# One plain feed-forward round per layer instead of two, with the output projection's accumulators held open between two passes

## The chip, the cores and the metric

The kernel runs on one core of a Trainium2 chip. The metric is the device time of one execution in microseconds (us); three executions of the kernel before took 1064.5 to 1064.76 us, median 1064.71 us. All times below are us from the start of the profiled span. PE is the matrix engine (TensorE), PEld its weight loads, DVE the vector engine (VectorE), ACT the scalar engine (ScalarE), POOL is GpSimd, SP the engine that issues most transfers.

## The reference, cut to what matters

Two identical layers run over one sequence of 512 frames of width 1024. A layer mixes three attention-like groups, projects their concatenated output back, and then applies a feed-forward of width 4096 with a squared ReLU:

```
x = x + concat(A, B, C) @ w_out
u = rms(x, norm2) @ w_ff1
x = x + square(relu(u)) @ w_ff2
```

with `rms(x, g) = x * rsqrt(mean(x*x) + 1e-6) * g`. Everything is float32. The change touches `concat(A, B, C) @ w_out` and the two feed-forward products.

## The kernel before

The activation `xT` lies transposed in SBUF: eight tiles of 128 features by 512 frames. Each float32 matrix product is made of three passes at a reduced input format: an operand is split into `hi` (a rounded copy) and `lo` (operand minus `hi`), and `mm3` (L262 to L265) issues hi·hi, hi·lo and lo·hi into one PSUM accumulator. For weights the split happens on the way: a weight tile of 128 x 1024 is loaded into a raw buffer, ACT copies it to `whi` (L205) and DVE writes `wlo = raw - whi` (L206). `jobs` is the list of weight tiles in the order of their use; `getjob` hands out the next, and `prep_ahead` prepares at most three (`HIB`) ahead, since `whi` and `wlo` have three buffers each: the copy for tile n waits until PE is done with tile n-3.

**Output projection** (`big_work`, L571 to L592). Its eight contraction tiles k are taken in three passes (`WPASS`: k 0 to 3, 4 and 5, 6 and 7), because the mixed output `yg` becomes ready in that order: tiles 6 and 7 come last, from `c_tail(0)` and `c_tail(1)`, which transpose `yts` (L1007, written by POOL at L1000) and split it. Each pass runs over four pairs of output tiles (`hf` 0 to 3) with two accumulators, and each accumulator is added into `xT` by DVE at the end of its pass (L587). After the last pass `xprep` writes `xh` and `xl`, the split, scaled input of the feed-forward (ACT L334, DVE L335). So one layer has 24 of the additions at L587.

**Feed-forward** (L1097 to L1383). The first matrix is taken in eight rounds of 512 output features. The first `NSTD` = 2 rounds are plain (`ff1_std`): four weight tiles per round, 48 matmuls of 128 x 256 each (8 pairs of k and feature half, two halves of the frames, three passes), 192 in all. The other rounds are Strassen-Winograd rounds (`ff1_st`): seven products of 24 matmuls each, 168 in all, from seven combinations of four weight blocks (`ORDER` = A11, S1, S2, A12, S4, S3, A22) and of the input's four blocks. S1 and S3 are summed by a second transfer that accumulates into the raw buffer (POOL's queue), S2 and S4 by DVE (L216, L220). The input's combinations are the tile `xbx`, written by `xsums` (ACT L354 and L363, DVE L356 to L375). A round ends with four blocks of squared ReLU in `ct`, whose combinations are split into `gx` and `yg` units for the second matrix (`csplit`, `n1_`, `n2_`, `tail_`; L1183 to L1205). Those of `tail_` are put off until the next round has begun (`late`, `flush`). The second matrix (`ff2`) uses Winograd products throughout, 14 for each pair of rounds, and adds each product into `xT` (`acc`, L1294). `ff_pairs` alternates one product of `ff2` with one of `ff1_st`. While the plain rounds run, `sqacc` sums the squares of `xT`, `xsums` runs, and `emit_r2` (L1121) makes the frame's normaliser: one all-ones matmul (L1123), then `nv`, Ln, Exp, and two DVE operations of a Newton step (L1130, L1131).

A scheduler fixes the order of the instructions on each engine when the program is built; each engine then runs its own list strictly in order.

## Time and profile before

| what | before |
|---|---|
| median of three runs | 1064.71 us |
| profiled execution, its own time | 1064.91 us |
| its span | 1063.1 us |
| PE instructions | 8768 matmuls |
| DMA moved | 151.86 MB |
| mean granted PE clock | 0.999 of full speed |

The span of the profiled execution is 1.8 us shorter than its time, and the execution took 0.2 us longer than the median. In layer 0 the output projection ends and the first plain round begins at about 222.7 us, the second plain round ends at about 267.2 us, and the feed-forward ends at about 546 us; layer 1 repeats the same stages some 525 us later. A busy share of PE counts pipelined matmuls that overlap, so it says that PE was never empty, not that it worked at its peak.

### The profile page before, as it was taken

The numbers are of one execution on the slowest core, as the hardware profiler recorded it, in microseconds if no ns is written. First come the engines' busy times: TensorE is split into PE (matmuls) and PEld (weight loads), VectorE is DVE, ScalarE is ACT, GpSimd is POOL, SyncE is SP. The second block draws the span as 40 slices with busy tenths as digits, with TensorE's granted clock in tenths as the row PEclk, the third lists the DMA queues.
The fourth block names the chain that finished last, engine by engine and source line by source line (L and its number), as shares of the span: only waits on it lengthen the run. The fifth ranks groups of instructions, "written<-read, shape, count | busy, mean of one in ns | idle before, by whom it ended". The sixth has DMA issues, their size and how long they took to land.

```text
span 1063.1 us, 21688 instructions
## 1 busy us (share of the span) xinstructions
PE 1054.7 (99%) x8768; PEld 1004.3 (94%) x8768; DVE 904.4 (85%) x1541; ACT 627.8 (59%) x1097; POOL 102.5 (10%) x154
## 2 busy tenths in 40 slices
PE   9999999999999999999999999999999999999998
PEld 8999977899999999999999998778999999999998
DVE  7696877899997988988977978678999888898898
ACT  6446655376666666567455467444766666666662
POOL 2030020100010000010001200101000101001000
PEclk9999999999999999999999999999999999999999
DMA  6523111165388677677135221213544877777742
GB/s 217 165 98 110 60 68 51 61 194 144 119 213 220 162 219 198 177 199 199 51 110 163 96 80 41 84 47 127 152 120 138 220 187 201 219 188 184 224 128 80
DMA packets 47365, 151.86 MB, mean 143 GB/s; under 512 B 5648, under 2 KB 8848, under 8 KB 47264
## 3 DMA queue, kind: packets, MB, share of 16 engines
q1 hardware_dynamic: 39056, 120.84, 33.8%
q0 software_dynamic: 8064, 29.36, 15.7%
q8 instruction: 69, 1.13, 0.4%
q14 instruction: 32, 0.26, 0.1%
q10 hardware_dynamic: 144, 0.26, 0.1%
HBM read 147.86 MB, written 2.13 MB: 141 GB/s over the span
## 4 chain that ended last, share of the span: by engine, by line
PE 86%; DVE 9%; ACT 3%; issue 1%; DMA 0%; SPq 0%; DVEq 0%
PE at L263 26%; PE at L264 26%; PE at L265 26%; DVE rt L726 2%; DVE wlo L206 2%; PE at L856 1%; PE at L898 1%; PE at L881 1%; ACT pe L769 1%; PE at L979 1%; DVE z L722 1%; DVE z L728 1%; PE at L756 1%; DMA raw<-in_w_in_dram 0%; DVE rb L407 0%
## 5 line engine op out<-in xcount | busy, mean ns | idle before, releaser
L205 ACT ACTIVATE whi<-raw 128x1024 fp32r<-128x1024 f32 (+1 forms) x130 | 136.2, 1048 | 114.3 <-PE at L264 87.3
L264 PE MATMUL at<-xhl,whi 128*128 128x256 f32 (+1 forms) x704 | 198.0, 281 | 0.0
L263 PE MATMUL at<-xhl,whi 128*128 128x256 f32 (+1 forms) x640 | 181.4, 283 | 0.0
L265 PE MATMUL at<-xhl,wlo 128*128 128x256 f32 (+1 forms) x640 | 180.4, 282 | 0.0
L206 DVE TENSOR_TENSOR wlo<-raw,whi 128x1024 fp32r<-128x1024 f32 (+1 forms) x130 | 157.2, 1209 | 26.8 <-ACT whi L205 26.5
L263 PE MATMUL at<-yg,whi 128*128 128x256 f32 (+1 forms) x592 | 179.8, 307 | 0.0
L265 PE MATMUL at<-yg,wlo 128*128 128x256 f32 (+1 forms) x592 | 178.4, 301 | 0.0
L264 PE MATMUL at<-yg,whi 128*128 128x256 f32 (+1 forms) x560 | 169.4, 303 | 0.0
L263 PE MATMUL at<-whi,xhl 128*128 128x256 f32 (+1 forms) x576 | 163.7, 284 | 0.2 <-ACT whi L205 0.2
L264 PE MATMUL at<-wlo,xhl 128*128 128x256 f32 (+1 forms) x576 | 161.2, 280 | 0.3 <-DVE wlo L206 0.3
L265 PE MATMUL at<-whi,xhl 128*128 128x256 f32 (+1 forms) x576 | 161.0, 280 | 0.1
L205 ACT ACTIVATE whi<-fraw 128x1024 fp32r<-128x1024 f32 x100 | 106.1, 1061 | 83.8 <-PE at L264 79.6
L206 DVE TENSOR_TENSOR wlo<-fraw,whi 128x1024 fp32r<-128x1024 f32 x100 | 121.9, 1219 | 26.2 <-ACT whi L205 25.7
L264 PEld LDWEIGHTS at<-xhl,whi 128*128 128x128 f32 x704 | 132.2, 188 | 1.8 <-issue 0.5
L263 PEld LDWEIGHTS at<-xhl,whi 128*128 128x128 f32 x640 | 120.2, 188 | 1.7 <-ACT ct L1232 0.5
L265 PEld LDWEIGHTS at<-xhl,wlo 128*128 128x128 f32 x640 | 120.1, 188 | 1.2
L263 PEld LDWEIGHTS at<-yg,whi 128*128 128x128 f32 x592 | 111.2, 188 | 5.6 <-issue 1.7
L265 PEld LDWEIGHTS at<-yg,wlo 128*128 128x128 f32 x592 | 111.1, 188 | 5.3
L263 PEld LDWEIGHTS at<-whi,xhl 128*128 128x128 f32 x576 | 109.1, 189 | 1.1 <-ACT whi L205 0.5
L264 PEld LDWEIGHTS at<-wlo,xhl 128*128 128x128 f32 x576 | 109.0, 189 | 0.6 <-DVE wlo L206 0.6
L265 PEld LDWEIGHTS at<-whi,xhl 128*128 128x128 f32 x576 | 109.1, 189 | 0.3 <-DVE xhl L335 0.3
L264 PEld LDWEIGHTS at<-yg,whi 128*128 128x128 f32 x560 | 105.2, 188 | 4.2 <-DVE yg L1009 0.5
(301 smaller groups left out, 2516.3 us busy)
## 6 DMA issues: line engine op xcount, KB each, us to landing
fraw<-in_w_dram SPq DMA_DIRECT2D x72, 512.0 KB, 4.4
raw<-in_w_dram SPq DMA_DIRECT2D x56, 512.0 KB, 4.3
raw<-in_w_in_dram SPq DMA_DIRECT2D x34, 512.0 KB, 3.3
fraw<-in_w_dram POOLq DMA_DIRECT2D x32, 512.0 KB, 6.5
raw<-in_w_out_dram SPq DMA_DIRECT2D x16, 512.0 KB, 3.2
xt<-in_w_dram SPq DMA_DIRECT2D x16, 512.0 KB, 6.0
raw<-in_w_dram POOLq DMA_DIRECT2D x14, 512.0 KB, 7.4
ms<-in_w_dram SPq DMA_DIRECT2D x12, 512.0 KB, 4.4
```

The costliest lines, as they stand in the source:

```text
L205: A.activation(hi[:, cs_], raw[:, cs_], AF.Copy)
L206: V.tensor_tensor(lo[:, cs_], raw[:, cs_], hi[:, cs_], ALU.subtract)
L263: T.matmul(o, sh, mh, start=first, stop=False, skip_group_check=skip)
L264: T.matmul(o, sh, ml, start=False, stop=False, skip_group_check=skip)
L265: T.matmul(o, sl, mh, start=False, stop=last, skip_group_check=skip)
L722: V.tensor_tensor(z10, z10, bc(rq), ALU.mult)
L726: V.tensor_tensor(r10[:, oo:oo + n, a:a + 32], z10[:, oo:oo + n, b:b + 32], tb(S_, n, a, a + 32), ALU.mult)
L728: V.tensor_tensor(zaq[t], ro[:, :640], rt[:, :640], ALU.add)
L756: T.matmul(sc[r][:, g * 256:g * 256 + nk], qTA[g][r * 64:(r + 1) * 64, c * P:(c + 1) * P], kTA[r * 64:(r + 1) * 64, k0:k0 + nk], start=Tru ...
L769: A.activation(pe[:, u, :nk], sc[u % 2][:, (u // 2) * 256:(u // 2) * 256 + nk], AF.Exp, bias=nmx[:, u:u + 1], accum_out=ssum[:, u:u + 1])
L856: T.matmul(sp[:, :nk], qTB[rs, pr, n * P:(n + 1) * P], kTB[rs, pr, :nk], start=True, stop=False)
L881: T.transpose(pt[:, b * P:(b + 1) * P], scs[r][:, b * P:(b + 1) * P], ident)
```

## The change

`NSTD` goes from 2 to 1 and `LEAD` from 0 to 7: the second round of each layer is now a Winograd round, and its seven products are all taken ahead of the first product of `ff2`. The work that lay beside the two plain rounds is dealt out anew: `xsums` runs in the four steps of the one plain round, `sqacc` and `emit_r2` are taken in the Winograd round that follows, and the two Newton operations move to `finish_r2`, at the end of the first `ff2`. The square of the plain round's second half no longer stands behind its ReLU but in `flush`, which the Winograd round calls after it has copied a bank (`A.activation(Y, X, AF.Copy)`); with the square go `n2_` and the release of the units. `bank(True)` picks a bank that has held a matmul before.

```
-NSTD = 2
+NSTD = 1
...
-    LEAD = 0
+    LEAD = 7
...
+            open_ = {}
+            for hf in range(3):
+                open_[hf] = [att() for _ in range(2)]
+                if hf != 1:
+                    ws = getjob()
+                for k in (4, 5):
+                    wo_part(open_[hf], ws[2 * (hf % 2) + k - 4], k, k == 4, False)
+                    if k == 5:
+                        done.add(f"wo1{hf}")
                     yield 1.31
+            for hf in (2, 0, 1, 3):
+                if hf == 3:
+                    open_[hf] = [att() for _ in range(2)]
+                if hf in (0, 3):
+                    ws = getjob()
+                for k in range(4 if hf == 3 else 6, 8):
+                    wo_part(open_[hf], ws[k - 4 if hf == 3 else (hf if hf < 2 else 1) * 2 + k - 6], k, hf == 3 and k == 4,
+                            k == 7)
...
+                wo_out(open_[hf], hf, True)
...
-        fill_to("wo1")
+        fill_to("wo11")
         c_tail(1)
+        fill_to("wo12")
         close_phase()
...
+        def finish_r2():
+            nv, lnv, r2 = (rr_[n] for n in ("nv", "lnv", "r2"))
             V.tensor_tensor(lnv, nv, r2, ALU.mult)
             V.scalar_tensor_tensor(r2, lnv, 2.0, r2, ALU.add, ALU.mult)
-            rr_.update(nv=nv, r2=r2)
...
+        def square(i):
+            A.activation(ct[:, 2 * i:2 * i + 2], ct[:, 2 * i:2 * i + 2], AF.Square)
+
         def flush():
             while late:
-                tail_(*late.pop(0))
+                s, rr, plain = late.pop(0)
+                if plain:
+                    square(1)
+                    if rr == NSTD - 1:
+                        units.extend(quads)
+                    n2_(s, rr)
+                tail_(s, rr)
...
-        for n_ in range(4 * NSTD):
-            next(gens[1])
+        for n_, (which, u) in enumerate([(1, None)] * 4 * NSTD + list(ff_pairs())):
+            next(gens[which])
             if n_ == 0:
+                xt_ = wt("xt", "xt")
+                bg = xsums(l, *(v3(xt_[:, i * S:(i + 1) * S], 256) for i in range(2)))
+            if n_ < 4:
+                next(bg)
+                next(bg)
+            if n_ == 4:
                 for kx in range(KT):
                     sqacc(kx, kx == 0)
-            if n_ == 3:
+                free_ff.append(xt_)
+            if n_ == 7:
                 emit_r2()
```

In the projection the first pass stays. Pass two now leaves the accumulators of `hf` 0, 1 and 2 open (six of the eight banks), pass three goes on in them in the order 2, 0, 1, and `hf` 3 takes its four contraction tiles in one go at the end. Three pairs are so added into `xT` once instead of twice: 18 additions per layer instead of 24. The host packs the weight tiles of `w_out` to match.

**Order on PE at the projection.** PE's list of layer 0 around the transposes of the last mixed tile (`yt` of `c_tail(1)`); `at` are PSUM banks, `yg` the mixed output, the number behind `whi` is the weight tile. Before:

```order
L263 MATMUL at_521_2838<-yg_91,whi_476_2624 128x512
L264 MATMUL at_521_2838<-yg_91,whi_476_2624 128x512
L265 MATMUL at_521_2838<-yg_91,wlo_477_2625 128x512
L1007 MATMUL at_522_2853<-ident_76,yt_493_2695 128x128 x4
L263 MATMUL at_530_2870<-yg_91,whi_512_2781 128x512
```

Now, 24 matmuls nearer to the program's start:

```order
L264 MATMUL at_515_2799<-yg_91,whi_419_2442 128x512
L265 MATMUL at_515_2799<-yg_91,wlo_420_2443 128x512
L1035 MATMUL at_516_2812<-ident_76,yt_493_2695 128x128 x4
L263 MATMUL at_517_2819<-yg_91,whi_476_2624 128x512
L264 MATMUL at_517_2819<-yg_91,whi_476_2624 128x512
```

The four transposes stood behind the second pass's last matmul with tile 476; they now stand ahead of its first.

**Order on DVE behind the plain rounds.** DVE's list of layer 0 from the last operation of `xsums` but one to the lo copies of the products that follow (`wlo` with the number of its tile, `ct` the blocks of the squared ReLU, `gx` and `yg` the units). Before, around the end of the first of two plain rounds:

```order
L206 TENSOR_TENSOR wlo_561_3253<-fraw_529_2869,whi_560_3252 128x1024
L356 SCALAR_TENSOR_TENSOR xbx_526_2866<-xt_555_3103,xbx_526_2866 128x512
L1199 SCALAR_TENSOR_TENSOR ct_528_2868<-ct_528_2868 128x512
L1200 TENSOR_TENSOR ct_528_2868<-ct_528_2868 128x512
L1184 TENSOR_TENSOR gx_527_2867<-ct_528_2868,gx_527_2867 128x1024 x2
L1130 TENSOR_TENSOR ms_525_2865<-ms_525_2865,r20_3237 128x512
L1205 SCALAR_TENSOR_TENSOR ct_528_2868<-ct_528_2868 128x512
L1131 SCALAR_TENSOR_TENSOR r20_3237<-ms_525_2865,r20_3237 128x512
L375 SCALAR_TENSOR_TENSOR xt_555_3103<-xT_89,pcol_106,xt_555_3103 128x256 x2
L1184 TENSOR_TENSOR yg_91<-ct_528_2868,gx_527_2867 128x1024
L356 SCALAR_TENSOR_TENSOR xbx_526_2866<-xt_555_3103,xbx_526_2866 128x512
L206 TENSOR_TENSOR wlo_563_3320<-raw0_73,whi_562_3319 128x1024
```

Now, around the end of the one plain round:

```order
L356 SCALAR_TENSOR_TENSOR xbx_524_2843<-xt_544_3013,xbx_524_2843 128x512
L206 TENSOR_TENSOR wlo_552_3217<-fraw_527_2846,whi_551_3216 128x1024
L1236 SCALAR_TENSOR_TENSOR ct_526_2845<-ct_526_2845 128x512
L1237 TENSOR_TENSOR ct_526_2845<-ct_526_2845 128x512
L206 TENSOR_TENSOR wlo_555_3275<-raw0_73,whi_554_3274 128x1024
L1221 TENSOR_TENSOR gx_525_2844<-ct_526_2845,gx_525_2844 128x1024 x2
L220 TENSOR_TENSOR fraw_527_2846<-raw0_73,fraw_527_2846 128x1024
L1242 SCALAR_TENSOR_TENSOR ct_526_2845<-ct_526_2845 128x512
L206 TENSOR_TENSOR wlo_557_3305<-fraw_527_2846,whi_556_3304 128x1024
L1221 TENSOR_TENSOR yg_91<-ct_526_2845,gx_525_2844 128x1024
L206 TENSOR_TENSOR wlo_559_3337<-raw2_75,whi_558_3336 128x1024
```

Between two halves of the same `ct` work there stood no lo copy before; now there are three, and a sum of weight blocks (L220), because the tiles are used up twice as fast. In both lists `L1236`/`L1199` and the two rows behind the first of them are the work of `n2_`, the rest of the `ct` rows that of `tail_`.

**Order on PE at the first product of `ff2`.** PE's list of layer 0 where the Winograd round ends (tile 562 is the first of `ff2`, tile 560 the last of the round):

```order
L264 MATMUL at_541_2957<-yg_91,whi_562_3408 128x256
L265 MATMUL at_541_2957<-yg_91,wlo_563_3409 128x256
L263 MATMUL at_541_2957<-yg_91,whi_562_3408 128x256
L264 MATMUL at_541_2957<-yg_91,whi_562_3408 128x256
L263 MATMUL at_538_2954<-xbx_524_2843,whi_560_3374 128x256
```

The scheduler has put the first 17 matmuls of the first `ff2` product ahead of the round's seventh product, and the other seven behind it.

More of the change, by code (lines that the diff above doesn't have):

```diff
@@ L572, in big_work, with wo_part @@
                 yield 1.31
-            for pi, (a, b) in enumerate(WPASS):
-                for hf in range(4):
-                    ps = [att() for _ in range(2)]
-                    if b - a == 4 or hf % 2 == 0:
-                        ws = getjob()
-                    for k in range(a, b):
-                        hi, lo = ws[k - a if b - a == 4 else hf % 2 * 2 + k - a]
-                        for j in range(2):
-                            cs_ = slice(j * P, (j + 1) * P)
-                            mm3(ps[j], hi[:, cs_], lo[:, cs_], yhi(k), ylo(k), k == a, k == b - 1)
-                        if k < b - 1:
-                            yield 1.31
-                    for j in range(2):
-                        kx = hf * 2 + j
-                        V.tensor_tensor(xT[:, kx], ps[j], xT[:, kx], ALU.add)
-                        if pi == len(WPASS) - 1:
-                            xprep(kx, g2(l, kx), xh, xl)
-                    if hf == 3:
-                        done.add(f"wo{pi}")
-                    yield 1.31
+            def wo_part(ps, tiles, k, first, stop):
+                hi, lo = tiles
+                for j in range(2):
+                    cs_ = slice(j * P, (j + 1) * P)
+                    mm3(ps[j], hi[:, cs_], lo[:, cs_], yhi(k), ylo(k), first, stop)
@@ new lines, in wo_out @@
+            def wo_out(ps, hf, full):
+                for j in range(2):
+                    kx = hf * 2 + j
+                    V.tensor_tensor(xT[:, kx], ps[j], xT[:, kx], ALU.add)
+                    if full:
+                        xprep(kx, g2(l, kx), xh, xl)
+            for hf in range(4):
+                ps = [att() for _ in range(2)]
+                ws = getjob()
+                for k in range(4):
+                    wo_part(ps, ws[k], k, k == 0, k == 3)
+                    if k < 3:
+                        yield 1.31
+                wo_out(ps, hf, False)
+                if hf == 3:
+                    done.add("wo0")
+                yield 1.31
@@ L1114, in trunk, with bank @@
         banks = deque(att() for _ in range(8))
-        def bank():
-            return banks.popleft()
+        full = set()
+        def bank(seeded=False):
+            b = next(b for b in banks if not seeded or id(b) in full)
+            banks.remove(b)
+            full.add(id(b))
+            return b
         rr_ = {}
@@ L1233, in ff1_std @@
                         banks.extend(ps)
-                        A.activation(ct[:, 2 * i:2 * i + 2], ct[:, 2 * i:2 * i + 2], AF.Square)
                         if i == 0:
+                            square(0)
                             csplit(s, rr)
@@ L1238, in ff1_std @@
                         else:
-                            if rr:
-                                units.extend(quads)
-                            n2_(s, rr)
-                            late.append((s, rr))
+                            late.append((s, rr, True))
                     yield
         def ff1_st(s, rr):
-            X, Y = bank(), bank()
+            X, Y = bank(), bank(True)
             prod1(X, 0)
@@ L1276, in ff1_st @@
             banks.append(X)
-            late.append((s, rr))
+            late.append((s, rr, False))
             if (s, rr) == (NS - 1, 1):
@@ L1359, in ff2 @@
                 if s == 0 and dg:
+                    finish_r2()
                     free_ff.append(ms_)
@@ L1365, in trunk @@
         bg = None
-        for n_ in range(4 * NSTD):
-            next(gens[1])
+        for n_, (which, u) in enumerate([(1, None)] * 4 * NSTD + list(ff_pairs())):
+            next(gens[which])
             if n_ == 0:
+                xt_ = wt("xt", "xt")
[4 more added lines that the diff above has]
+            if n_ == 4:
                 for kx in range(KT):
                     sqacc(kx, kx == 0)
-            if n_ == 3:
+                free_ff.append(xt_)
+            if n_ == 7:
                 emit_r2()
-            if n_ == 1:
-                xt_ = wt("xt", "xt")
-                bg = xsums(l, *(v3(xt_[:, i * S:(i + 1) * S], 256) for i in range(2)))
-            if bg is not None:
-                next(bg, None)
-                next(bg, None)
-        free_ff.append(xt_)
-        for which, u in ff_pairs():
-            next(gens[which])
         close_phase()
@@ L1417, in _layout @@
         c = w_out[l].reshape(D, 4, 256).transpose(1, 0, 2)
-        t = [tiles(c, a, b - a) for a, b in WPASS]
-        wo.append(cc([t[0]] + [cc([t_[0::2], t_[1::2]], 2) for t_ in t[1:]], 0))
+        t, u, v = (tiles(c, a, b - a) for a, b in WPASS)
+        two = [cc(p, 1) for p in ((u[0], u[1]), (u[2], v[2]), (v[0], v[1]), (u[3], v[3]))]
+        wo.append(cc([t, np.stack(two)], 0))
     wo = np.stack(wo)
```

8 lines of the change are left out of this document (added).

## The prediction

> **What bounds the kernel now.** I read the page first, for the engine that fills the span.
>
> ```profile
> PE 1054.7 (99%) x8768; PEld 1004.3 (94%) x8768; DVE 904.4 (85%) x1541; ACT 627.8 (59%) x1097; POOL 102.5 (10%) x154
> PE 86%; DVE 9%; ACT 3%; issue 1%; DMA 0%; SPq 0%; DVEq 0%
> ```
>
> PE is never empty and carries 86% of the chain that ended last. A matmul less is worth its issue interval, if whoever feeds PE keeps up. Who that is I read from the stretches that change, in layer 0: the two plain rounds, and the first products behind them.
>
> ```profile
> core 0: us, PE busy (x) PEld busy (x) DVE busy (x) ACT busy (x) POOL busy (x), PEclk, DMA share, GB/s
> 222.60:244.60 22.00, 22.00 (x196) 22.00 (x195) 21.83 (x37) 15.57 (x26) 1.88 (x2) 1.00 0.57 145
> 244.60:267.30 22.70, 22.70 (x197) 22.22 (x196) 22.70 (x32) 14.45 (x20) 1.72 (x2) 1.00 0.49 117
> 267.30:305.50 38.20, 38.20 (x339) 38.20 (x338) 35.31 (x39) 25.76 (x32) 2.57 (x3) 1.00 0.51 151
> ```
>
> The reader is to see the DVE column: 44.5 of 44.7 us in the two plain rounds. DVE is full there, although its share of the whole span is 85%. PE still does not wait, because the backlog is covered by weight tiles prepared ahead:
>
> ```profile
> 250.97 1.06 ACT L205 ACTIVATE whi<-raw 128x1024 fp32r<-128x1024 f32 x1
> 256.04 1.21 DVE L206 TENSOR_TENSOR wlo<-raw,whi 128x1024 fp32r<-128x1024 f32 x1
> ```
>
> This `wlo` lay behind four microseconds of other DVE work, was done at 257.25, and PE came to its tile, the last of the eight plain ones, at 261.8 (222.82, its start of the first, plus seven tiles of 5.44 us and 0.86 us, both worked out below). The cover was 4.5 us, and a plain tile lasts 5.4 us on PE. A Winograd tile lasts half of that and takes the same DVE work, so halving the plain rounds spends that cover.
>
> **What the change takes from PE.** The price of a matmul:
>
> ```profile
> 223.04 0.28 PE L265 MATMUL at<-xhl,wlo 128*128 128x256 f32 x1
> ...
> 244.46 0.28 PE L265 MATMUL at<-xhl,wlo 128*128 128x256 f32 x1
> 244.58 1.02 PE L1123 MATMUL at<-accs,ones_m 128*128 128x512 f32 x2
> ...
> 245.55 0.28 PE L264 MATMUL at<-xhl,whi 128*128 128x256 f32 x1
> ```
>
> These are the 3rd and the 192nd matmul of the first plain round: 21.42 us / 189 = 0.1133 us. A plain tile of 48 is 5.44 us, a Winograd product of 24 is 2.72 us, and a round falls from 192 to 168. **PE saves 24 x 0.1133 = 2.72 us per layer, 5.44 us in all.** The sum of squares (L1123) costs 245.55 - 0.11 - 244.58 = 0.86 us and stays. The projection has as many matmuls as before.
>
> **What it adds on the way to PE.** A Winograd round in place of a plain one has three more weight tiles (three whi, three lo copies), two sums of weight blocks on DVE and two more 512-wide additions on DVE (L1307, L1313). What these cost is the distance between starts in a full queue:
>
> ```profile
> 242.18 0.88 DVE L364 SCALAR_TENSOR_TENSOR xt<-xT,pcol,xt 128x256 f32<-128x256 f32 x2
> 242.98 0.87 DVE L368 SCALAR_TENSOR_TENSOR xt<-xT,pcol,xt 128x256 f32<-128x256 f32 x2
> ...
> 257.17 1.28 DVE L1293 SCALAR_TENSOR_TENSOR xT<-xT,ms 128x512 f32<-128x512 f32 x2
> 258.38 1.22 DVE L206 TENSOR_TENSOR wlo<-raw,whi 128x1024 fp32r<-128x1024 f32 x1
> 259.51 0.68 DVE L1293 SCALAR_TENSOR_TENSOR xT<-xT,ms 128x512 f32<-128x512 f32 x1
> ```
>
> So 0.40 us for 256 elements (242.18 to 242.98, two), 0.60 for 512 (257.17 to 258.38, two), and 1.135 for 1024 (256.04 to 257.17, 258.38 to 259.51). The round adds 5 x 1.135 + 2 x 0.60 = 6.9 us to DVE and takes 2.7 us of PE time away, where DVE had 0.2 us left. The six additions per layer saved in the projection (6 x 0.60 = 3.6 us) lie ahead of this, where DVE waits for PE:
>
> ```profile
> 210.62 1.37 DVE L587 TENSOR_TENSOR xT<-at,xT 128x512 f32<-128x512 f32 x2 [1.08 <-PE at L265]
> 214.82 1.29 DVE L587 TENSOR_TENSOR xT<-at,xT 128x512 f32<-128x512 f32 x2 [0.82 <-PE at L265]
> ```
>
> I count them at nothing: the last lo copies ahead of the feed-forward are held by `whi` buffers that PE frees, not by DVE.
>
> **The transposes moved forward.** They now come 24 matmuls of 512 earlier.
>
> ```profile
> 206.34 0.39 PE L263 MATMUL at<-yg,whi 128*128 128x512 f32 x1
> ...
> 208.38 0.39 PE L263 MATMUL at<-yg,whi 128*128 128x512 f32 x1
> ...
> 211.10 0.60 PE L1007 MATMUL at<-ident,yt 128*128 128x128 f32 x4
> 204.57 1.17 POOL L1000 TENSOR_TENSOR yt<-hs,co 128x64 f32<-128x64 f32 x4 [3.93 <-DVE hs L996]
> ...
> 267.29 1.06 ACT L205 ACTIVATE whi<-fraw 128x1024 fp32r<-128x1024 f32 x1
> 268.39 1.23 DVE L206 TENSOR_TENSOR wlo<-fraw,whi 128x1024 fp32r<-128x1024 f32 x1 [0.57 <-ACT whi L205]
> ```
>
> Nine of them take 2.04 us (206.34 to 208.38), so PE arrives at 211.10 - 24 x 0.227 = 205.66, and POOL's `yt` ends at 205.74. PE and all projection matmuls behind it wait 0.1 us and the handover. For POOL to PE no row shows that; it lies between what ACT to DVE takes (267.29 + 1.06 to 268.39, 0.04 us) and one more of POOL's four multiplications (1.17 / 4 = 0.3 us). So the wait is 0.1 to 0.4 us; I take **0.2 us**, nearer to the row of a handover. The split of `yt` then has 18 matmuls, 4 us, of cover.
>
> **DVE's queue against PE, layer 0.** I walk the new order with these prices. PE enters the plain round 0.2 us later, at 223.02 (223.04 less two intervals, plus 0.2), and leaves it at 223.02 + 21.76 = 244.78. Product n in PE's new order (the sum of squares behind the fourth) could start at 244.78 + 2.72 (n - 1), from the fifth on plus 0.86, and asks for its lo copy two matmuls later, 0.23 us.
>
> ```profile
> 222.64 1.05 ACT L205 ACTIVATE whi<-raw 128x1024 fp32r<-128x1024 f32 x1
> 233.72 0.58 ACT L1232 ACTIVATE ct<-at 128x512 f32<-128x512 f32 x1
> 234.20 1.05 ACT L205 ACTIVATE whi<-fraw 128x1024 fp32r<-128x1024 f32 x1
> 235.15 0.58 ACT L1232 ACTIVATE ct<-at 128x512 f32<-128x512 f32 x1
> ```
>
> - The lo copy of the third plain tile waits for its `whi`, whose buffer the projection's end frees (before at 222.64): 222.64 + 0.2 + 1.05 = 223.9. From there to the last operation of `xsums` DVE's list has 5 of 1024, 19 of 512, 14 of 256: 22.7 us, no gap: 246.6.
> - The next lo copy (tile 552) waits for ACT, which behind PE's 244.78 has a ReLU, an `xbx` copy that itself waits for DVE, a ReLU and the `whi`: at 0.48 for a 512 ReLU and 1.05 for a `whi`, done at 247.5. DVE idles 0.9 us.
> - To the lo copy of the seventh product in PE's order (tile 562, the first of `ff2`): 10 of 1024 and 7 of 512, 15.6 us, and one wait of 0.55 us where the sum L220 goes to ACT for its `whi` and back with only one DVE operation between: **263.7**. PE asks at 244.78 + 6 x 2.72 + 0.86 + 0.23 = 262.2. It waits **1.5 us**. The PE order helps nothing here: the product that is ready (tile 560) stands behind.
> - From there to the lo copy of tile 592 (the 23rd product): 25 of 1024 and 26 of 512, 44.0 us: 307.7. PE without any wait: 244.78 + 22 x 2.72 + 0.86 + 0.23 = 305.7. Lateness by then **2.0 us** in all. Behind that tile the eight multiplications by `nv` (512 each) are over and DVE gains.
>
> The deferred square costs nothing by itself: ACT's list has it ahead of the bank's copy, done at about 248.5, where DVE comes to `n2_` at 248.7. ACT then has 0.1 us to spare at one place: the copy into `ct` block 1 must wait for the lo split of `tail_`, and the product that goes on in the copied bank waits for it. I take 0 there. The Newton operations move behind the worst place, but tile 592's lo copy still has one of them ahead (0.6 us, in the 44.0).
>
> Loads: three more tiles per layer.
>
> ```profile
> fraw<-in_w_dram SPq DMA_DIRECT2D x72, 512.0 KB, 4.4
> fraw<-in_w_dram POOLq DMA_DIRECT2D x32, 512.0 KB, 6.5
> ```
>
> A block and its accumulating second need 11 us. The four `fraw` buffers are free once the transposes are done, and the first sum is asked for at about 239, so nothing waits; the DMA share in the windows above was 0.5.
>
> **Sum.** Per layer -2.72 + 0.2 + 2.0 = -0.5 us; twice: -1.0. From the profiled execution's 1064.91 that is 1063.9; the median stood 0.2 below this execution, so **1063.7 us** on the runs' scale, a gain of 0.1%. About 0.2% (2.1 us) is what a measurement can tell from none.
>
> **Rivals.**
> 1. *DVE's gaps close.* The 1.45 us of DVE waits that I counted and the POOL wait may be less, when ACT comes a little earlier. Without any, the lateness at tile 592 is 0.55 us, per layer -2.17, in all -4.3: 1060.4. For it: in the two windows of the plain rounds DVE had 0.2 us of gaps. Against it: both gaps are chains (ReLU to `whi` to lo; sum to `whi` to lo) that the old order didn't have under such pressure. With the cases between, 0.2.
> 2. *The lo copies are no limit at all*: full 5.4 us, 1059.3. DVE would have to come to tile 592 at 305.7 instead of 307.7, with 82.2 us of work behind its start at 223.9: 0.4 us less than the work alone; 0.05.
> 3. *Slower: ACT and DVE wait for each other in the first Winograd round.* The place is the chain square, `n2_`, lo splits, copy into `ct`, next product. It decides as soon as that copy ends after about 259.4, where PE comes to the sixth product; every later microsecond is PE's. The price of such a wait:
>
> ```profile
> 290.15 1.23 DVE L206 TENSOR_TENSOR wlo<-fraw,whi 128x1024 fp32r<-128x1024 f32 x1 [1.17 <-ACT whi L205]
> ```
>
> With two more of 1.17 us the lateness is 4.3, per layer +1.8, in all +3.6: 1068.3. For it: no slack on either engine there. Against it: most of DVE's waits in this list fall behind its own backlog. 0.14.
> 4. *Each DVE instruction costs its whole duration, not its spacing.* The rows above show 0.68 and 1.22 us long instructions 0.60 and 1.135 us apart, so 0.08 us of each lies under the next. By whole durations the 35 + 33 instructions from 247.5 to tile 592 cost 68 x 0.08 = 5.4 us more, per layer +4.9, in all 1074.7; 0.01. The Trainium skill, VectorE: DVE Perf Modes, section Terms, says that the pipe is flushed after every DVE operation and that the "next op can't issue until 8-slice pipe empties". This case's rows at 257.17 and 258.38 don't show it at the length of the rows (0.60 us apart), so the measurement decides.
>
> **How the numbers follow.** The forecast, 1063.7, stands for a lateness between 1.5 and 3.5 us per layer (1062.6 to 1066.8): 0.6. Rivals 1 (0.2) and 2 (0.05) lie below that, 3 (0.14) and 4 (0.01) above. So faster by over 0.2%: 0.25; within: 0.6; slower: 0.15. The range takes in rival 1 and leaves out 2, 3 and 4, 2 in 10: 1060.3 to 1066.8.
>
> **What would show it.** PE 48 matmuls fewer; DMA some 3.1 MB more; L582's group 36 instead of 48. Right: idle time ahead of PE at the first L265 on `gx`, released by DVE `wlo`, near 262 us, and of the same kind up to 308 us, 2 us per layer; at L1035 0.2 us released by POOL; DVE without gaps from 223 to 320 but for two, at 247 and 255. Wrong: PE without idle time from 245 to 310 (rival 1 or 2); PE waiting for ACT at `xbx` products before 262 us (rival 3); DVE starts 0.68 us apart (rival 4); any wait for DMA.

## The result, and the profile after

| | before | after |
|---|---|---|
| median | 1064.74 us (4 executions, 1064.5 to 1064.8) | 1083.61 us (4 executions, 1082.89 to 1083.92) |
| ratio, 95% interval | | 1.0177 [1.016, 1.0193] |
| span of the profiled execution | 1063.1 us | 1081.2 us |
| DMA moved | 151.86 MB | 154.99 MB |

The changed kernel is 18.9 us slower; forecast were 1063.7 us and a range of 1060.3 to 1066.8. (Ratios leave out executions over 1.5% above the fastest of their kernel; where a kernel's executions fall on steps, all of them are listed below.)

The page of after, first the busy time and then the chain:

```profile
PE 1070.3 (99%) x8720; PEld 1018.2 (94%) x8720; DVE 908.7 (84%) x1539; ACT 635.7 (59%) x1113; POOL 105.6 (10%) x158
PE 80%; DVE 14%; ACT 3%; issue 2%; DMA 0%; SPq 0%; DVEq 0%
```

PE has the 48 matmuls fewer that were forecast, and is busy 15.6 us longer: 1070.3 against 1054.7. Fewer matmuls in more busy time is not idle time; each takes longer. The waits of PE's weight loads in layer 0 of after (engine, line, releaser: us in total, times, longest):

```profile
PEld at L265 <- DVE wlo L206: 1.2, 2, 1.1
PEld at L263 <- ACT at L1291: 0.3, 1, 0.3
PEld at L263 <- issue: 0.2, 1, 0.2
PEld at L264 <- issue: 0.2, 1, 0.2
PEld at L263 <- ACT whi L205: 0.2, 1, 0.2
```

That is 2.1 us, about what the prediction had. So the windows, for the count of matmuls in equal stretches (columns as in the prediction). Before, far behind the change:

```profile
284.00:334.00 50.00, 50.00 (x444) 50.00 (x443) 42.01 (x45) 31.83 (x39) 4.32 (x5) 1.00 0.76 205
950.00:1000.00 50.00, 50.00 (x444) 50.00 (x443) 45.47 (x48) 31.19 (x37) 4.34 (x5) 1.00 0.66 180
```

After:

```profile
222.10:244.00 21.90, 21.90 (x195) 21.90 (x194) 21.76 (x37) 15.71 (x25) 0.86 (x1) 1.00 0.34 102
284.00:334.00 50.00, 50.00 (x427) 50.00 (x427) 44.84 (x50) 30.13 (x37) 5.18 (x6) 1.00 0.77 212
802.00:836.00 34.00, 34.00 (x302) 34.00 (x301) 34.00 (x39) 21.80 (x26) 1.21 (x2) 1.00 0.48 131
950.00:1000.00 50.00, 50.00 (x427) 50.00 (x426) 44.63 (x48) 31.26 (x38) 4.35 (x5) 1.00 0.65 171
```

PE is never empty in any of them and the granted clock is 1.00 throughout, but 427 matmuls run where 444 ran. Some three of each count straddle the edges: 50 / 441 = 0.1134 us a matmul, 50 / 424 = 0.1179. The plain round (195 in 21.9 us) and 802 to 836 us still run at the short spacing. It changes within a few matmuls; the timeline of PE in after (start, length, line):

```profile
265.01 0.28 PE L265 MATMUL at<-yg,wlo 128*128 128x256 f32 x1
265.13 0.28 PE L263 MATMUL at<-yg,whi 128*128 128x256 f32 x1
265.24 0.28 PE L264 MATMUL at<-yg,whi 128*128 128x256 f32 x1
265.35 0.36 PE L263 MATMUL at<-xbx,whi 128*128 128x256 f32 x1
265.56 0.28 PE L264 MATMUL at<-xbx,whi 128*128 128x256 f32 x1
265.67 0.28 PE L265 MATMUL at<-xbx,wlo 128*128 128x256 f32 x1
265.79 0.28 PE L263 MATMUL at<-xbx,whi 128*128 128x256 f32 x1
265.91 0.28 PE L264 MATMUL at<-xbx,whi 128*128 128x256 f32 x1
```

Up to 265.35 the starts are 0.113 us apart, but for a few. The weight load of the matmul at 265.35, the first on `xbx`, came about 0.1 us late, the next matmul starts 0.20 us behind it instead of 0.11, and from there the starts are 0.118 apart: 2453 matmuls on end, until the next layer's attention breaks the stream. In layer 1 the same begins with a wait of 0.20 us at 836.98 us and holds for 2038 matmuls to the end. DVE's addition and PE's weight load at both places:

```profile
264.59 0.69 DVE L1313 TENSOR_TENSOR ct<-at,ct 128x512 f32<-128x512 f32 x1
265.33 0.19 PEld L263 LDWEIGHTS at<-xbx,whi 128*128 128x128 f32 x1
836.16 0.70 DVE L1313 TENSOR_TENSOR ct<-at,ct 128x512 f32<-128x512 f32 x1
836.98 0.19 PEld L263 LDWEIGHTS at<-xbx,whi 128*128 128x128 f32 x1 [0.20 <-issue]
```

The view shows no idle time for the first load and names no releaser for the second ("issue"). Both are the first of a Winograd round's seventh product, which goes on in the PSUM bank that the sixth product's addition L1313 reads, and they come 0.05 and 0.12 us behind that addition's end. By this order PE waited there for a bank that a late DVE had only just read, and not for a `wlo`. Behind the long wait for `wlo` at 263.53 the spacing was still the short one.

Intervals between starts in both feed-forwards, from the two traces, add up: 4558 long ones in after (0.116 us and up) are 20.3 us too much, some 125 of them in before 0.6 us: **+19.8 us**. Longer gaps (waits, and the sum of squares, which both have): 5.9 us against 1.2, **+4.7**. 48 matmuls fewer: **-5.4**. Together +19.0, where the spans differ by 18.1. Most of the rest lies outside the feed-forwards: the first one begins 0.7 us earlier in after (0.6 of this is gained in the first 17 us of the program), and the stretch between the two is 0.1 us shorter.

### The profile page after: what moved, and what is told of

Same layout as the page of the kernel before. It is cut to its first block, busy times and chain, and to the rows that moved or that the text cites. A ratio compares the mean times of both kernels' runs of the same rounds, so it can differ in the third digit from the quotient of the medians.

```text
span 1081.2 us, 21622 instructions
## 1 busy us (share of the span) xinstructions
PE 1070.3 (99%) x8720; PEld 1018.2 (94%) x8720; DVE 908.7 (84%) x1539; ACT 635.7 (59%) x1113; POOL 105.6 (10%) x158
## 2 busy tenths in 40 slices
DMA packets 48228, 154.99 MB, mean 143 GB/s; under 512 B 5744, under 2 KB 8944, under 8 KB 48128
## 4 chain that ended last, share of the span: by engine, by line
PE 80%; DVE 14%; ACT 3%; issue 2%; DMA 0%; SPq 0%; DVEq 0%
PE at L263 24%; PE at L265 24%; PE at L264 24%; DVE wlo L206 3%; DVE rt L754 2%; PE at L884 1%; PE at L926 1%; DVE accs L330 1%; PE at L909 1%; PE at L784 1%; DVE xhl L335 1%; ACT whi L205 1%; PE at L1007 1%; DVE z L756 1%; DVE z L750 1%
## 5 line engine op out<-in xcount | busy, mean ns | idle before, releaser
L205 ACT ACTIVATE whi<-raw 128x1024 fp32r<-128x1024 f32 (+1 forms) x136 | 142.3, 1046 | 114.1 <-PE at L264 85.1
L206 DVE TENSOR_TENSOR wlo<-raw,whi 128x1024 fp32r<-128x1024 f32 (+1 forms) x136 | 164.6, 1211 | 32.0 <-ACT whi L205 31.7
L263 PE MATMUL at<-yg,whi 128*128 128x256 f32 (+1 forms) x592 | 183.0, 311 | 0.0
L265 PE MATMUL at<-yg,wlo 128*128 128x256 f32 (+1 forms) x592 | 180.5, 305 | 0.0
L264 PE MATMUL at<-xhl,whi 128*128 128x256 f32 (+1 forms) x624 | 178.0, 285 | 0.0
L264 PE MATMUL at<-yg,whi 128*128 128x256 f32 (+1 forms) x560 | 171.2, 306 | 0.0
L263 PE MATMUL at<-xhl,whi 128*128 128x256 f32 (+1 forms) x560 | 161.0, 288 | 0.0
L265 PE MATMUL at<-whi,xhl 128*128 128x256 f32 (+1 forms) x576 | 160.5, 279 | 0.5 <-DVE xhl L335 0.5
L265 PE MATMUL at<-xhl,wlo 128*128 128x256 f32 (+1 forms) x560 | 160.3, 286 | 0.2 <-DVE wlo L206 0.2
L206 DVE TENSOR_TENSOR wlo<-fraw,whi 128x1024 fp32r<-128x1024 f32 x102 | 125.0, 1225 | 26.7 <-ACT whi L205 26.6
L263 PE MATMUL at<-xbx,whi 128*128 128x256 f32 x448 | 126.1, 281 | 0.3
L265 PE MATMUL at<-xbx,wlo 128*128 128x256 f32 x448 | 125.6, 280 | 0.0
L264 PE MATMUL at<-xbx,whi 128*128 128x256 f32 x448 | 125.5, 280 | 0.0
L264 PEld LDWEIGHTS at<-xhl,whi 128*128 128x128 f32 x624 | 117.1, 188 | 1.8 <-issue 0.5
L265 PEld LDWEIGHTS at<-yg,wlo 128*128 128x128 f32 x592 | 113.0, 191 | 5.4
L263 PEld LDWEIGHTS at<-yg,whi 128*128 128x128 f32 x592 | 111.1, 188 | 5.8 <-issue 1.7
L265 PEld LDWEIGHTS at<-whi,xhl 128*128 128x128 f32 x576 | 108.3, 188 | 0.9 <-DVE xhl L335 0.9
```

Source lines behind the costliest of these rows:

```text
L205: A.activation(hi[:, cs_], raw[:, cs_], AF.Copy)
L206: V.tensor_tensor(lo[:, cs_], raw[:, cs_], hi[:, cs_], ALU.subtract)
L263: T.matmul(o, sh, mh, start=first, stop=False, skip_group_check=skip)
L264: T.matmul(o, sh, ml, start=False, stop=False, skip_group_check=skip)
L265: T.matmul(o, sl, mh, start=False, stop=last, skip_group_check=skip)
```

## The experiments

The stream means here PE's unbroken row of 128x256 matmuls, and a break is whatever interrupts its even spacing. Theory A: the 128x256 matmuls have two steady spacings, 0.1133 and 0.1178 us; a break in the stream, such as a wait, can leave it in either, and it stays there until the next break. Theory B (rival): the long spacing belongs to what the changed kernel does all the time, its traffic, order or buffers, and a wait costs its own length.

**1. Waits put into the kernel before: spoiled by an address.** In the middle of a product of `ff2` (called second-layer products in the expectations) ACT reads one column of the PSUM bank, so PE's next matmul into it must wait; two such places, then 24, then 24 with a short added matmul behind each.

```
+        hold_ = sm.tile([P, 1], F32, tag="hold", name=f"hold{l}")
...
+                if hold and kk == 1:
+                    A.activation(hold_, bk[:, :1], AF.Copy)
```

> The kernel before, with one added ACT read of one PSUM column in the middle of the third second-layer product of each layer (the next matmul into that bank has to wait for it): two short PE waits, at about 278 and 803 us, all else as before. Theory A (the spacing of the 128x256 matmuls has two steady values, 0.1133 and 0.1178 us, and a PE wait can leave the stream in either, until the next break): each wait costs its own length, 0.5 to 1.5 us, and, where it leaves the slow spacing, also about 2200 matmuls x 0.0045 = 10 us to the end of that layer's feed-forward; so 1066, 1076 or 1086 us, and every stretch of the trace wholly at one of the two values. Theory B (the slow spacing belongs to something that the changed kernel does all the time: its traffic, its order, its buffers): 1065.5 to 1067.5 us, and 0.1133 throughout.

> The kernel before, with the same short PE wait at twelve places of each layer's feed-forward (three in each of four groups of second-layer products). Theory A: 24 throws; in the traces so far 4 of 9 waits in the feed-forward left the slow spacing, so about 0.44 x 4500 matmuls x 0.0045 = 9 us beside the waits' own lengths (24 x 0.5 to 1.0 = 12 to 24 us): 1086 to 1098 us, stretches between waits wholly at 0.1133 or 0.1178. Theory B: the waits alone, 1077 to 1089 us, and 0.1133 in all stretches.

> The run with 24 waits, and in each case one 128x128 fp32 matmul of ones on ones into the next fresh bank (its sum is overwritten), two products after the wait. Theory A with the rider that such a matmul brings the stream back to 0.1133: stretches from each added matmul to the next wait all fast, the slow share at most some 40 matmuls behind each wait (2 us in all), and with 24 x 0.25 = 6 us for the added matmuls about 1 us less to 3 us more than the run without them, depending on how much of that was slow. If the added matmul resets nothing: the time of the run without them + 6 us, and slow stretches that run through it.

Measured: 1081.71 us (ratio 1.016 [1.014, 1.018]), 1087.83 us (1.0218 [1.0197, 1.0238]) and 1092.13 us (1.0258 [1.0237, 1.0278]). But the spacing was a mixture of 0.113 to 0.125 us from 267 us on, ahead of the first added wait. The scratch tile had moved the feed-forward's buffers by 160 bytes. Neither theory is tested by these three.

**2. The address alone.** The feed-forward has an unused tile of 40 floats ahead of its buffers.

```
-    FFP = {"pad": (40, 1), "xbx": (8 * D, 1), ...
+    FFP = {"pad": (48, 1), "xbx": (8 * D, 1), ...
```

> The kernel before, with 32 bytes more of unused memory ahead of the feed-forward's buffers (the unused tile of 40 floats has 48), nothing else. The scratch tile of the three runs with added ACT reads had moved these buffers by 160 bytes as well, and there the spacing was mixed (mean 0.1167 us, single intervals from 0.113 to 0.125) from 267 us on, ahead of the first added wait. If the place of the buffers does this: about 2 x 2300 matmuls x 0.0034 = 16 us, 1080 us. If the waits did it: 1064.7 us and 0.1133 throughout.

1085.62 us, ratio 1.0197 [1.0177, 1.0218]. Its windows, the second plain round and then the Winograd products:

```profile
250.00:265.00 15.00, 15.00 (x135) 15.00 (x134) 15.00 (x21) 8.90 (x11) 1.72 (x2) 1.00 0.69 159
284.00:334.00 50.00, 50.00 (x426) 50.00 (x425) 40.28 (x42) 30.80 (x37) 4.32 (x5) 1.00 0.73 195
```

The plain rounds, whose input lies elsewhere, keep the count of before (135 in 15 us); behind them the count is that of the long spacing, without any wait. It is not the same state: single intervals of the products on the moved buffers spread from 0.115 to 0.124 us, where the long stretches of after have 0.117 to 0.119. So addresses alone can cost as much, in another way. It is not the change's way: before and after have all these buffers at the same addresses.

**3. The wait again, at unchanged addresses** (the read goes into the unused tile itself), at one place in each layer, then in layer 1 alone.

```
+                if hold and kk == 1:
+                    A.activation(pad_[:, :1], bk[:, :1], AF.Copy)
```

> The kernel before, with one added ACT read of one PSUM column in the middle of the third second-layer product of each layer, as in the first run of this kind, but written into a tile that exists already, so that every address is that of before. Theory A (a PE wait leaves the stream of 128x256 matmuls at 0.1133 or at 0.1178 us, and it stays there): 0.4 us for each wait, and 10 us more for each that leaves the slow spacing: 1065.5, 1075.5 or 1085.5 us, all stretches at one of the two values. Theory B (a wait costs its own length): 1065.5 us and 0.1133 throughout.

> The kernel before, with the added ACT read of one PSUM column (a PE wait) in layer 1 alone, at about 805 us, every address and all of layer 0 as before. Theory A, with the pick differing from execution to execution: each execution at 1065.5 or at 1075.5 us (2236 matmuls x 0.00445 = 10 us), nothing between. Theory B: all at 1065.5 us.

The first gave 1066.52 and 1086.12 us in its two executions, the second 1064.65 to 1066.23 in ten and 1075.4 us in one. The added wait in the second (weight loads of PE):

```profile
805.58 0.19 PEld L263 LDWEIGHTS at<-yg,whi 128*128 128x128 f32 x1 [0.66 <-ACT pad L1151]
```

The profiled execution of each stayed at 0.1133 behind it. So the same program, with one wait of 0.66 us, ends about 1 or about 10.7 us late. That is theory A's grid, and no constant cost of the program gives it, nor does the clock, which was granted at 0.999 to 1.000 in all of these executions. The executions off the short step are told apart by their time alone, since none of them was traced.

**4. A break without a wait.** One 128x128 matmul of ones on ones into a bank that the next product overwrites, in the kernel before.

```
                 Z[dg] = bank()
+                if (s, dg) == (0, 0):
+                    T.matmul(Z[dg][:, :P], ones_m, ones_m, start=True, stop=True)
                 prod2(Z[dg], s, 3)
```

> The kernel before, with one 128x128 fp32 matmul of ones on ones ahead of the third second-layer product of each layer (about 278 and 803 us; its sum is overwritten), no wait. In the run of the changed kernel with sixteen such matmuls each of them changed the state of the stream, from slow to fast and from fast to slow. Theory A in the form that any break in the stream, this short one too, picks the spacing anew, here always the other one: from there to the end of each feed-forward 0.1178, 2 x 10 us, about 1085 us. If the breaks pick at random: 1065, 1075 or 1085 us. If the added matmul always brings 0.1133: 1065.2 us.

1084.49 us, ratio 1.0187 [1.0166, 1.0207]. PE at the added matmul (L1318):

```profile
277.65 0.28 PE L264 MATMUL at<-xbx,whi 128*128 128x256 f32 x1
277.76 0.28 PE L265 MATMUL at<-xbx,wlo 128*128 128x256 f32 x1
277.88 0.38 PE L1318 MATMUL at<-ones_m 128*128 128x128 f32 x2
278.01 0.36 PE L263 MATMUL at<-gx,whi 128*128 128x256 f32 x1
278.21 0.28 PE L264 MATMUL at<-gx,whi 128*128 128x256 f32 x1
278.33 0.28 PE L265 MATMUL at<-gx,wlo 128*128 128x256 f32 x1
278.45 0.28 PE L263 MATMUL at<-gx,whi 128*128 128x256 f32 x1
```

0.11 us apart ahead of it, 0.12 behind it, to the end of each feed-forward. 0.2 us of work in each layer cost 20.0 us (from 1064.49), and nothing else of the kernel was touched. So the long spacing needs nothing that only the changed kernel has, and theory B falls here. That a wait leads into it too is seen in the traces of the kernels that have waits (at 265 and 837 us above, and in 7 and 8).

**5. Two breaks in a row.** The same at 278 us and again 574 matmuls later.

> The kernel before, with two of the 128x128 fp32 matmuls of ones in each layer: one at about 278 us, as in the run that gave 1084.5 us, and one ahead of the first product of the next group, 574 matmuls later (about 345 us; in layer 1 at 803 and 870). If each such break turns the spacing over (what 16 of 16 of them did so far): fast, slow for 574 matmuls, fast again, so 1064.7 + 2 x 574 x 0.00445 + 4 x 0.22 = 1070.7 us. If a break in a steady stream always leaves it slow: 1085 us. If it picks at random: spread over 1070 to 1085.

Four executions, 1070.28 to 1070.57 us, ratio 1.0055 [1.0041, 1.0069]: 0.2 us from the figure expected. Windows ahead of, between and behind the two:

```profile
250.00:275.00 25.00, 25.00 (x223) 25.00 (x222) 24.39 (x32) 16.04 (x20) 1.72 (x2) 1.00 0.47 111
284.00:334.00 50.00, 50.00 (x427) 50.00 (x426) 40.63 (x43) 30.75 (x37) 4.31 (x5) 1.00 0.73 200
350.00:400.00 50.00, 50.00 (x444) 50.00 (x443) 46.01 (x49) 31.04 (x37) 4.32 (x5) 1.00 0.70 186
```

Short, long, short. Such a matmul turns the spacing over.

**6. The same matmuls in the changed kernel**: eight in each layer, then one in each layer's long stretch (the rider, in the first expectation, is the guess that such a matmul brings the short spacing back).

> The changed kernel, with the same 128x128 fp32 matmul of ones ahead of eight second-layer products of each layer. Theory A with the rider: the slow stretches (2453 matmuls from 265 us, 2038 from 837 us, 20 us in all) end at the next added matmul, at most 30 us on: 1083.6 - 18 + 16 x 0.25 = 1069 to 1071 us. Theory B, or no reset: 1086 to 1088 us with the slow spacing in the same stretches.

> The changed kernel, with one such matmul in each layer, in its slow stretch: in layer 0 at about 278 us, in layer 1 at about 879 us. If a break picks the other spacing: slow only from 265 to 278 and from 837 to 879 us, some 465 of the 4491 slow matmuls: 1083.6 - 17.9 + 0.5 = 1066 us. At random: 1066, 1075 or 1084 us. Theory B: 1084 us.

The run with sixteen: 1070.66, 1077.7, 1077.76 and 1078.32 us; the rider was wrong, they turn the spacing over. Over these traces all 22 that fell into a stream without a wait did so. The run with two: ten executions, at 1066.01, 1066.24, 1066.47, 1066.83 and 1068.24; 1075.31, 1075.97 and 1077.31; 1081.35 and 1081.51 us: the three steps of none, one or two long layers. The profiled one, of 1079.8 us span, had the short spacing ahead of the added matmul (82 in 9 us) and the long one behind it:

```profile
268.00:277.00 9.00, 9.00 (x82) 9.00 (x81) 9.00 (x10) 7.82 (x10) 0.55 (x1) 1.00 0.56 118
284.00:334.00 50.00, 50.00 (x427) 50.00 (x427) 45.15 (x51) 30.25 (x37) 5.18 (x6) 1.00 0.81 216
```

So here the wait at 265 us had left the short spacing, in the same instructions in which it left the long one in after. One program has executions 15 us apart, all at a granted clock of 0.999 to 1.000.

**7. The changed kernel again**, unchanged.

> The changed kernel unchanged, for the spread of its executions. The four so far gave 1082.9 to 1083.9 us, and the profiled one was slow from 265 and from 837 us on. Theory A with a pick at random at each wait: now and then an execution in which one layer or both go on at 0.1133, at about 1074 or at 1063.6 us (the time of the run with two added matmuls, 1066.0 us in its best executions, less the 465 matmuls that these leave slow, 2.1 us, and their own 0.4 us). Theory A with the pick set by the program: all at 1083 to 1084 us.

1081.82, 1082.03, 1083.52 and 1084.26 us (ratio 1.017 [1.0155, 1.0185]): none on a lower step. Its trace is long from 307.8 us in layer 0, behind a wait that the first trace does not have, and from 836.1 us in layer 1. In layer 0 it was still short behind the waits at 265 and 302 us; the one that turned it, of less than 0.1 us, is a wait for `wlo` at the 23rd product, at 307.57 us. With several late places there are several picks, and the last one holds. A stream that was left short comes sooner to the next late place and waits again; the first trace, long from 265 us, has no later wait in layer 0. That favours the long spacing, but it does not settle why both layers of both traces had it: in the run with two added matmuls layer 1 was still short behind its waits at 837 and 843 us.

**8. Part of the change alone**: the projection's new order with `NSTD = 2` and `LEAD = 0`. It keeps more than was meant: `sqacc` later, the Newton step at the end of the first `ff2`, the square behind the copy.

```
-NSTD = 1
+NSTD = 2
...
-    LEAD = 7
+    LEAD = 0
```

> The new order of the output projection (six accumulators open between two passes, the transposes 24 matmuls earlier) with two plain rounds and no lead, so without the move of the plain round. By the prediction: 0.2 us more for each layer at the transposes, 1065.1 us. Theory A: it has no wait in the feed-forward before 531 us, so 0.1133 as before, and the same time. If the projection part itself costs (other idle time ahead of the feed-forward): above 1066 us.

1068.31, 1077.42, 1084.18 and 1086.99 us. The expectation took it to have no wait in the feed-forward ahead of 531 us; the trace, of the slowest of the four, has such waits in both layers. A weight load and, behind it, a matmul of layer 0:

```profile
301.00 0.19 PEld L265 LDWEIGHTS at<-gx,wlo 128*128 128x128 f32 x1 [1.07 <-DVE wlo L206]
305.24 0.36 PE L263 MATMUL at<-xbx,whi 128*128 128x256 f32 x1 [1.46 <-DVE ct L1313]
```

The spacing is short up to the second one and long from it to the end of the layer (2134 matmuls), at the addresses of before and with two plain rounds. The times cannot price the projection, but the trace shows a wait leading into the long spacing without the missing plain round. The second wait is again one for the bank that L1313 reads.

**9. What before owes to its own matmul of ones** at the start of each feed-forward.

```
-                if (s, rr, i) == (0, 0, 0):
-                    T.matmul(ps[0][:, :P], ones_m, ones_m, start=True, stop=True)
```

> The kernel before without the 128x128 matmul of ones that it has at the start of each feed-forward (its sum is overwritten). If the spacing is picked by breaks alone, the break between the projection's 512-wide matmuls and the feed-forward remains, and the plain rounds may come out at either value: 0.2 us less in each layer, or 190 matmuls x 0.00445 = 0.85 us more, and if the break at the sum of squares turns over or keeps what it finds, up to 10 us more in each layer: 1064.3 to 1086 us. If that matmul has no part in it: 1064.3 us.

1066.13 us, ratio 1.0014 [1.0005, 1.0023]. The first plain round, and the second behind the sum of squares:

```profile
224.00:244.00 20.00, 20.00 (x173) 20.00 (x172) 19.66 (x33) 13.47 (x22) 1.50 (x2) 1.00 0.57 146
250.00:265.00 15.00, 15.00 (x135) 15.00 (x134) 15.00 (x22) 8.96 (x11) 1.72 (x2) 1.00 0.69 157
```

173 where before has 178 in the same window: the first round is long, and the 128x512 fp32 matmul of the sum of squares brings the short spacing back. The line looks useless and is worth 1.5 us.

**10. Taking the loss back with that larger matmul**, first where the smaller ones stood, then behind the last wait seen (one of 0.86 us in each layer).

The edit of the second run:

```
+                if (s, dg) == (1, 0):
+                    T.matmul(X[dg], ones_m, rr_["r2"], start=True, stop=True)
                 prod2(X[dg], s, 0)
```

> The changed kernel with a 128x512 fp32 matmul (0.86 us, the size of the sum of squares) at the two places where the earlier run had a 128x128 one. If the larger one always leaves the fast spacing: all executions at 1083.6 - 17.9 + 1.7 = 1067.4 us or up to 2 us less. If it turns the spacing over, or picks at random: executions between 1067 and 1085 us in steps of about 9. If it changes nothing: 1085 us where the waits left both layers slow.

> The changed kernel with one 128x512 fp32 matmul (0.86 us) in each layer ahead of the first product of the second group (about 345 and 880 us), behind all the waits that were seen, which end at 308 and 843 us. If such a matmul always leaves the fast spacing (nomark_before: slow to fast in both layers; mark_after512: slow to fast once): all executions fast from there on, 1063.6 + 1.7 + up to 2.7 us of slow matmuls ahead of it in layer 0 and 2.9 in layer 1: 1065.3 to 1071 us, with no execution above. If it turns over or picks at random: executions up to 1084 us.

1077.46, 1083.46, 1085.56 and 1087.3 us; then 1078.52, 1079.26, 1079.44 and 1084.48 us. In the second trace it left layer 0 long (427 in 50 us, as ahead of it) and turned layer 1 to the short spacing:

```profile
350.00:400.00 50.00, 50.00 (x427) 50.00 (x427) 44.47 (x46) 29.92 (x36) 4.33 (x5) 1.00 0.65 178
805.00:855.00 50.00, 50.00 (x427) 50.00 (x426) 49.97 (x56) 33.23 (x40) 3.46 (x4) 1.00 0.65 172
885.00:935.00 50.00, 50.00 (x443) 50.00 (x443) 45.75 (x48) 31.35 (x38) 4.34 (x5) 1.00 0.67 179
```

No sure repair: over all traces, where no wait fell beside it, such a matmul kept the short spacing, and turned the long one in four of six cases. The first of the two traces has more: layer 0 went from the short to the long spacing at 302.5 us, at the start of a Winograd round's seventh product, with no wait in view and no interval over 0.122 us:

```profile
280.00:300.00 20.00, 20.00 (x179) 20.00 (x178) 20.00 (x24) 10.76 (x13) 0.86 (x1) 1.00 0.58 161
305.00:325.00 20.00, 20.00 (x172) 20.00 (x171) 18.40 (x19) 12.66 (x15) 1.73 (x2) 1.00 0.93 255
```

The addition that frees this product's bank ended 0.12 us ahead of its weight load, so a wait of a few ns may hide there; that is not shown. Four other traces have one change without a break each, between 534 and 541 us, where the next layer's products begin. At unmoved addresses all the rest come at a wait or at a matmul of another shape.

**11. Fewer waits, by moving DVE work to POOL**: the seven additions of the sum of squares, or the eight multiplications by `nv`.

```
-            V.tensor_tensor(sq_acc["t"], sq_acc["t"], sq, ALU.add)
+            (G if "sq" in phase else V).tensor_tensor(sq_acc["t"], sq_acc["t"], sq, ALU.add)
...
-                V.scalar_tensor_tensor(t_, t_, -1.0, bc_("nv"), ALU.mult, ALU.mult)
+                G.tensor_tensor(t_, t_, bc_("nv"), ALU.mult)
+                V.scalar_tensor_tensor(t_, t_, -1.0, q2(bk), ALU.mult, ALU.subtract if i else ALU.add)
...
```

> The changed kernel, with the seven additions for the sum of squares in each feed-forward on POOL instead of DVE: 7 x 0.60 = 4.2 us less in DVE's queue ahead of the first lo copies of the Winograd round, which were 2 us late. If POOL is fast enough (under 2 us for an addition), PE waits less at 262 us in each layer (1.06 us at one place in the profiled execution of the changed kernel) or not at all. Theory A: without any wait left, fast throughout, 1060 to 1062 us; with a single one left, that or 9 to 20 us more. Theory B: 1081 to 1084 us.

> The changed kernel with the eight multiplications by the norm (128x512) in each layer on POOL instead of DVE, 8 x 0.60 = 4.8 us less in DVE's queue from 260 us on. The wait of 1.06 us at 262 us should shrink to about 0.4, the later ones (302, 308, 836 us) go; the waits at 249 and 256 us stay. Theory A: executions on the steps fast/slow for each layer: 1062.5 us where the last wait left both fast, 10 us more for each layer left slow. Theory B: 1081 us.

1072.9, 1081.31, 1082.72 and 1090.62 us; and 1078.07, 1078.43, 1078.53 and 1089.21 us. Both made the waits longer. With the additions, which take POOL 1.5 us each, ACT's squares wait for POOL and PE waits 3.2 us for `xhl`. With the multiplications, DVE's own operations grew while POOL ran (260 to 276 us):

```profile
262.63 0.68 DVE L1307 TENSOR_TENSOR ct<-at,ct 128x512 f32<-128x512 f32 x1
264.32 2.29 DVE L206 TENSOR_TENSOR wlo<-fraw,whi 128x1024 fp32r<-128x1024 f32 x1
266.53 1.76 DVE L1233 TENSOR_TENSOR ct<-ct 128x512 f32<-128x512 f32 x1
```

The lo copy took 2.29 instead of 1.22 us, and PE waited 3.74 us for it. Behind that wait the granted clock fell:

```profile
266.00:272.00 6.00, 5.34 (x25) 5.34 (x26) 6.00 (x5) 1.26 (x2) 6.00 (x4) 0.50 0.01 2
```

Some 23 matmuls of each layer start 0.213 us apart there, 4.7 us in all. A second wait of 2 us follows, at 278 us and 810 us, and behind it the trace shows the short spacing in both layers, but for some 100 matmuls at the end of layer 0. So 1078 us is this kernel with hardly any long matmuls: the longer gaps (15.5 us against 1.2 in before) and the low clock eat the gain. No version here beats the kernel before.

## Why the prediction was wrong, step by step

- **Right: the matmuls.** 8720, 48 fewer; DMA 3.13 MB more. The additions at L582 are 32 and not 36, since the fourth pair is also added once (16 additions a layer, not 18); nothing hung on it.
- **Too high: the projection.** Forecast 0.2 us more a layer, at the transposes; the trace shows no idle time ahead of L1035, and from 17 us to the feed-forward of layer 0 the two traces agree within 0.1 us.
- **Right: DVE's two gaps.** Forecast 0.9 us at 247 and 0.55 at 255, and no other from 223 to 320 us. DVE in after has these two alone:

```profile
247.21 1.23 DVE L206 TENSOR_TENSOR wlo<-fraw,whi 128x1024 fp32r<-128x1024 f32 x1 [0.74 <-ACT whi L205]
255.31 1.23 DVE L206 TENSOR_TENSOR wlo<-fraw,whi 128x1024 fp32r<-128x1024 f32 x1 [0.53 <-ACT whi L205]
```

- **Right: where the lo copies come late.** Forecast: PE waits from 262.2 to 263.7 us at the first L265 on `gx`, for `wlo`, and 2.0 us by tile 592, whose lo copy was to come at 307.7. PE's weight loads in after:

```profile
249.61 0.19 PEld L263 LDWEIGHTS at<-xbx,whi 128*128 128x128 f32 x1 [0.32 <-ACT at L1291]
256.59 0.19 PEld L265 LDWEIGHTS at<-xhl,wlo 128*128 128x128 f32 x1 [0.17 <-DVE wlo L206]
263.53 0.19 PEld L265 LDWEIGHTS at<-gx,wlo 128*128 128x128 f32 x1 [1.06 <-DVE wlo L206]
```

  The forecast wait ends at 263.53 and is 1.06 us long, since PE came to it later, behind smaller waits. The second trace has the other end of the queue: its wait for `wlo` at the 23rd product ends at 307.57. The copy of the bank (L1291), which I had taken at 0 for its 0.1 us of slack on ACT, cost 0.32: the mechanism of rival 3, at a seventh of its price. The wait for the bank that L1313 reads is in no term of the prediction.
- **Wrong: "a matmul less is worth its issue interval".** The step took 0.1133 us as a property of the matmul, read from a stream without breaks, and a wait at its own length. So the sum (-2.72 + 0.2 + 2.0 a layer) has no term for the matmuls that remain; it takes them as unchanged. The runs show that the interval is a state of the stream, and that a wait can change it for thousands of matmuls. In the first trace two waits of 0.1 and 0.2 us did so, and 4.45 ns for each matmul behind them made most of 19.8 us: more than three times the 5.4 us at stake. Neither was a wait that the prediction had (both are at the bank of L1313); in layer 0 of the second trace it was one that it had, for `wlo` at 307.6. The profile of before had the warning in it, at its one wait late in layer 0 (from 532 to 545 us 112 matmuls run, where 118 ran from 515 to 528), and I did not look for it.
- **The sum without that step** comes out: 1083.6 - 19.8 = 1063.8 us, forecast 1063.7. An agreement to 0.1 us is in part luck, since the terms differ: the waits were 2.2 and 2.7 us in the two layers instead of 2.0, and the projection cost nothing instead of 0.2. The best executions of the kernel with two added matmuls say the same: 1066.0, less some 465 long ones that these leave (2.1 us) and their own 0.4 us, is 1063.5; this is worked out, not timed.
- **The rivals** all priced PE's waits by their length, or DVE's work that leads to them. None had matmuls that themselves come further apart, so the range was too narrow on the side of slower.

## What to carry to other kernels

In a kernel that PE bounds, count matmuls in equal windows, before and after a wait: busy share and granted clock do not show a longer spacing. A short wait in a long unbroken stream of small matmuls may cost far more than its length, so a change that trades matmuls for waits is safest with slack enough to have none at all, and its time should be taken from many executions. Keep the addresses of matmul operands fixed when an experiment adds a buffer.

## What the runs showed of the hardware

- Two steady spacings of 128x256 matmuls at a granted clock of 1.00: 0.1133 and 0.1178 us, each for up to some 2500 matmuls without a change. The Trainium skill, TensorE: Matmul & The Clock Gate, section "Wait — 56ns, not 53.3ns?", gives one warm interval for back-to-back matmuls, columns / 2.4 GHz and about 2.5 ns, which for 256 columns is an estimate of 0.109 us. Here every matmul has a weight load of its own (8720 of each in after), and the traces show two other intervals; these decide. What inside PE holds the state is open.
- A 128x128 fp32 matmul turned the state over, 22 times of 22; a wait picked either; in five places of the traces it changed with neither beside it.
- Operand buffers moved by 32 bytes gave a mean spacing like the long one, without a break, but with single intervals of 0.115 to 0.124 us: 1085.62 us.
- Behind a PE wait of 3.7 us the granted clock was 0.50 from 266 to 272 us, and 128x256 matmuls started 0.213 us apart; behind waits of up to 2 us it stayed at 1.00.
- While POOL multiplied, DVE operations on two SBUF operands took 1.76 us instead of 0.69 and 2.29 instead of 1.22, one with a PSUM operand (L1307) 0.68 as ever. The Trainium skill, GPSIMD Engine Reference, section Specifications, has GpSimd's SBUF interfaces shared with VectorE, in contention with DVE instructions that have two SBUF inputs; the trace agrees.
